# Subtracting the low part of every fourth weight chunk on GpSimd

## The chip, the cores and the metric

The kernel runs on one core of a Trainium2 chip. The time is device time in microseconds of one execution, compared by the median of several runs. Below, PE is TensorE (PEld its weight loads), DVE is VectorE, ACT is ScalarE, POOL is GpSimd and SP is SyncE, which issues the weight loads.

## What is computed

Two layers of an encoder over one sequence of 256 tokens of width 2048, in float32. Each layer has a mixer (an mLSTM group, a retention group and an attention group, side by side, from one projection of width 4432) and a feed-forward part of width 8192:

```
for l in range(DEPTH):
    h = _rms(x, g_mix[l])
    x = x + _mixer(h, cos, sin, w_in[l], ...)
    u = _rms(x, g_ffn[l])
    x = x + jnp.square(jax.nn.relu(u @ w_ff1[l])) @ w_ff2[l]
return _rms(x, g_final)
```

All weights together are some 390 MB, each read once. The matrix products dominate.

## The kernel before

**Split weights.** PE multiplies in a float32 form with fewer bits (`F32R`). To keep accuracy each operand is split in two: a high part, the value rounded to `F32R`, and a low part, the value minus the high part. Each product then has three matmuls: high by high, activation-high by weight-low, activation-low by weight-high. The activations are split once when they are made; the weights are split on the fly, and this is what the change is about.

**The weight stream.** `weight_plan` (line 47) lists all weights in the order in which PE wants them, and the host lays them out that way as 737 chunks, nearly all of 128 partitions by 1024 elements (512 KB). Class `Stream` (line 209) moves them. `load` (line 219) issues one DMA for a chunk on SP into one of `NRAW` = 4 raw buffers. `prep` (line 229) makes the two parts of chunk i: ACT copies the raw chunk to `whi` (line 237), DVE subtracts it from the raw chunk into `wlo` (line 238). There are `NHL` = 4 buffers of each, so chunk i has the buffers of chunk i - 4. After each `prep` the load of chunk i + 4 is issued, into the raw buffer that chunk i gives free; it waits for both the copy and the subtraction. `get(i)` (line 243), called when PE's code comes to chunk i, first calls `prep` up to chunk i + 2, so chunk i + 2's copy waits until PE has read the last of chunk i - 2 from the same buffer, and the two parts are made some two chunks ahead of their use.

**The order of the work.** Everything stands in the order in which the Python code emits it, engine by engine; no scheduler moves it. The main line of code runs the big products chunk by chunk: `nat` (line 411, weights as the moving operand), `stat` (line 416, weights as the stationary operand) and `ff_tile` (line 1066). All other work of the mixer (norms, gates, softmax, heads) is in generators that `pump` (line 379) advances by a step here and there between the matmuls. Each engine works off its queue in order, so a subtraction on DVE can stand behind an evacuation that waits for PE.

**The feed-forward part.** `ff1` (line 1082) takes four chunks for two tiles of 128 hidden units; each tile is evacuated by `ff_evac` (line 1052): ACT copies one half of the PSUM bank (line 1061), DVE adds the other (1062) and squares (1063), ACT and DVE split the result (325, 330). `ff2` (line 1099) takes four chunks for one block of 512 output columns, and `ev_x` (line 1034) adds the block to x on DVE. Per layer 32 ff1 groups and 32 ff2 blocks alternate, after four ff1 groups at the start and with four ff2 blocks at the end. A round is one ff1 group and one ff2 block, eight chunks. The feed-forward chunks begin at number 113 in layer 0 and 481 in layer 1, and every group of four begins at a number that leaves 1 when divided by 4.

**POOL.** It fills two buffers: `krl` at the start (line 291) and `rq` once in each layer (line 886). Nothing else stands in its queue besides a few constants.

Of the kernel before, what the change touches and what calls it, by code (L numbers as in the profile page):

```python
# [10 lines left out]
F32 = mybir.dt.float32  # L11
# [3 lines left out]
ALU = mybir.AluOpType  # L15
# [193 lines left out]
class Stream:  # L209
# [19 lines left out]
    def prep(self, upto):  # L229
        while self.nprep < min(upto, len(self.sizes)):  # L230
            i = self.nprep
            f = self.sizes[i]
            self.load(i + 1)
            raw = self.raw.pop(i)
            hi = self.pool.tile([P, CH], F32R, name=f"whi{i}", tag="whi", bufs=NHL)
            lo = self.pool.tile([P, CH], F32R, name=f"wlo{i}", tag="wlo", bufs=NHL)
            self.nc.scalar.activation(hi[:, :f], raw[:, :f], AF.Copy)  # L237
            self.nc.vector.tensor_tensor(lo[:, :f], raw[:, :f], hi[:, :f].bitcast(F32), op=ALU.subtract)  # L238
            self.parts[i] = (hi, lo)
            self.nprep += 1  # L240
            self.load(i + 1 + NRAW)
# [983 lines left out]
```

## Time and profile before

| | us |
|---|---|
| median of 3 runs | 2163.01 |
| lowest and highest | 2162.09 to 2163.02 |
| the profiled execution | 2164.72 |
| its span in the profile | 2162.9 |
| granted clock of PE, mean | 0.999 |

The profile lists busy time by engine, groups of equal instructions by source line ("L238 DVE ... wlo<-wraw,whi x737" is the subtraction), and for each group the idle time of its engine just before it and what ended that idle time. The timeline gives start and length of instructions, with equal neighbours merged ("x3"). Tile names are without buffer numbers; since chunks are copied, subtracted and used in order, the n-th instruction of line 237 or 238 belongs to chunk n, counted from 0.

### The profile page before, as it was taken

The numbers are of one execution on the slowest core, as the hardware profiler recorded it, in microseconds if no ns is written. First come the engines' busy times: TensorE is split into PE (matmuls) and PEld (weight loads), VectorE is DVE, ScalarE is ACT, GpSimd is POOL, SyncE is SP. The second block draws the span as 40 slices with busy tenths as digits, with TensorE's granted clock in tenths as the row PEclk, the third lists the DMA queues.
The fourth block names the chain that finished last, engine by engine and source line by source line (L and its number), as shares of the span: only waits on it lengthen the run. The fifth ranks groups of instructions, "written<-read, shape, count | busy, mean of one in ns | idle before, by whom it ended". The sixth has DMA issues, their size and how long they took to land.

```text
span 2162.9 us, 29276 instructions
## 1 busy us (share of the span) xinstructions
PE 2144.4 (99%) x11280; PEld 1837.5 (85%) x11280; DVE 1355.2 (63%) x2019; ACT 1047.5 (48%) x1534; POOL 4.1 (0%) x7
## 2 busy tenths in 40 slices
PE   8999999999999999999999999999999999999998
PEld 7898888888888888888888988888888888888887
DVE  5767565665656566565666676756565656656565
ACT  6645655544434444444556456555444444444444
POOL 0000000000000000000000000000000000000000
PEclk9999999999999999999999999999999999999999
DMA  7544455565565556565565444555555565555554
GB/s 212 186 144 159 153 175 185 175 199 190 189 200 179 202 185 196 187 202 179 188 185 171 131 166 137 186 183 193 187 191 199 179 203 183 197 187 201 177 204 164
DMA packets 111356, 395.20 MB, mean 183 GB/s; under 512 B 12904, under 2 KB 14056, under 8 KB 111088
## 3 DMA queue, kind: packets, MB, share of 16 engines
q1 hardware_dynamic: 109072, 389.90, 55.1%
q10 hardware_dynamic: 2144, 3.43, 0.4%
q8 instruction: 88, 1.44, 0.3%
q14 instruction: 52, 0.43, 0.1%
HBM read 391.17 MB, written 2.12 MB: 182 GB/s over the span
## 4 chain that ended last, share of the span: by engine, by line
PE 94%; DVE 2%; ACT 1%; DMA 1%; issue 1%; ACTq 0%; SPq 0%; DVEq 0%
PE pm L336 57%; PE f L336 33%; DMA wraw<-in_w_dram 1%; PE sc L336 1%; DVE wlo L238 1%; PE o L336 1%; ACT whi L237 1%; PE num L336 0%; PE xt L333 0%; PE ry L336 0%; PE pt L333 0%; PE st L336 0%; ACT junk L306 0%; DVE mqk L767 0%; DVE mqk L757 0%
## 5 line engine op out<-in xcount | busy, mean ns | idle before, releaser
L238 DVE TENSOR_TENSOR wlo<-wraw,whi 128x1024 fp32r<-128x1024 f32 (+2 forms) x737 | 875.0, 1217 | 269.8 <-ACT whi L237 268.2
L237 ACT ACTIVATE whi<-wraw 128x1024 fp32r<-128x1024 f32 (+2 forms) x737 | 750.5, 1048 | 332.8 <-PE pm L336 289.3
L336 PE MATMUL f<-xT,whi 128*128 128x512 f32 x2048 | 712.0, 392 | 0.0
L336 PE MATMUL f<-xT,wlo 128*128 128x256 f32 x2048 | 552.1, 280 | 0.0
L336 PEld LDWEIGHTS f<-xT,whi 128*128 128x128 f32 x2048 | 379.4, 188 | 77.0
L336 PE MATMUL pm<-wlo,hhi 128*128 128x512 f32 (+1 forms) x1040 | 401.6, 386 | 0.6 <-DVE wlo L238 0.6
L336 PE MATMUL pm<-whi,hhi 128*128 128x512 f32 (+1 forms) x1040 | 402.1, 387 | 0.0
L336 PE MATMUL pm<-whi,hlo 128*128 128x512 f32 (+1 forms) x1040 | 401.2, 386 | 0.0
L336 PEld LDWEIGHTS f<-xT,wlo 128*128 128x128 f32 x2048 | 385.0, 188 | 11.3 <-DVE wlo L238 0.8
L336 PE MATMUL pm<-whi,xT 128*128 128x512 f32 (+1 forms) x896 | 290.2, 393 | 2.3 <-ACT whi L237 1.8
L1061 ACT ACTIVATE fr<-f 128x256 f32<-128x256 f32 x128 | 49.2, 385 | 374.7 <-PE f L336 374.7
L336 PEld LDWEIGHTS pm<-wlo,hhi 128*128 128x128 f32 x1040 | 195.4, 188 | 40.3 <-DVE wlo L238 1.0
L336 PEld LDWEIGHTS pm<-whi,hlo 128*128 128x128 f32 x1040 | 195.4, 188 | 39.7
L336 PEld LDWEIGHTS pm<-whi,hhi 128*128 128x128 f32 x1040 | 195.4, 188 | 37.1
L336 PEld LDWEIGHTS pm<-whi,xT 128*128 128x128 f32 x896 | 166.7, 189 | 35.2 <-ACT whi L237 2.1
L1062 DVE TENSOR_TENSOR fr<-f,fr 128x256 f32<-128x256 f32 x128 | 54.3, 424 | 218.2 <-ACT fr L1061 218.2
L1034 DVE SCALAR_TENSOR_TENSOR xx<-pm,rs,xx 128x512 f32<-128x512 f32 x126 | 90.1, 750 | 143.1 <-PE pm L336 143.1
L336 PE MATMUL pm<-wlo,xT 128*128 128x512 f32 (+1 forms) x448 | 173.0, 386 | 3.5 <-DVE wlo L238 3.5
L325 ACT ACTIVATE hhi<-fq 128x256 fp32r<-128x256 f32 x128 | 53.5, 418 | 126.8 <-DVE fq L1063 126.8
L336 PEld LDWEIGHTS pm<-wlo,xT 128*128 128x128 f32 x448 | 84.6, 189 | 20.6 <-DVE wlo L238 5.8
L336 PE MATMUL pm<-whi,yhi 128*128 128x512 f32 x256 | 101.5, 397 | 0.0
L336 PE MATMUL pm<-whi,ylo 128*128 128x512 f32 x256 | 99.8, 390 | 0.0
(238 smaller groups left out, 1616.4 us busy)
## 6 DMA issues: line engine op xcount, KB each, us to landing
wraw<-in_w_dram SPq DMA_DIRECT2D x723, 512.0 KB, 4.2
wraw<-in_w_dram SPq DMA_DIRECT2D x10, 504.0 KB, 6.8
wt<-mx_rows ACTq DMA_DIRECT2D x8, 256.0 KB, 3.8
out_dram<-xx SPq DMA_DIRECT2D x8, 256.0 KB, 2.9
xx<-in_x_dram SPq DMA_DIRECT2D x3, 512.0 KB, 8.3
gf<-in_gfin_dram ACTq DMA_DIRECT2D x1, 1024.0 KB, 9.1
xx<-in_x_dram SPq DMA_DIRECT2D x2, 256.0 KB, 4.0
wraw<-in_w_dram SPq DMA_DIRECT2D x2, 256.0 KB, 5.3
```

Of the source, the lines that this page charges most:

```text
L237: self.nc.scalar.activation(hi[:, :f], raw[:, :f], AF.Copy)
L238: self.nc.vector.tensor_tensor(lo[:, :f], raw[:, :f], hi[:, :f].bitcast(F32), op=ALU.subtract)
L325: A.activation(hi, src, AF.Copy, **({"scale": g[0]} if g else {}))
L336: T.matmul(ps, lhsT=lhsT, rhs=rhs, start=start, stop=stop)
L1034: V.scalar_tensor_tensor(x[t][:, xs], ps[t], scale[:, t:t + 1], x[t][:, xs], op0=ALU.mult, op1=ALU.add)
L1061: A.activation(r, ps[:, S:], AF.Copy)
L1062: V.tensor_tensor(r, ps[:, :S], r, op=ALU.add)
```

## The change

Chunks whose number leaves 3 when divided by 4 have their low part subtracted on POOL; the instruction, its inputs and its output are the same. These are 184 of the 737 chunks.

```
             self.nc.scalar.activation(hi[:, :f], raw[:, :f], AF.Copy)
-            self.nc.vector.tensor_tensor(lo[:, :f], raw[:, :f], hi[:, :f].bitcast(F32), op=ALU.subtract)
+            eng = self.nc.gpsimd if i % 4 == 3 else self.nc.vector
+            eng.tensor_tensor(lo[:, :f], raw[:, :f], hi[:, :f].bitcast(F32), op=ALU.subtract)
             self.parts[i] = (hi, lo)
```

Later lines of the file move down by one. Since the buffers of a chunk are chosen by its number, one of the four `wlo` buffers is now written by POOL alone. PE's first matmul on such a low part, and the load into such a raw buffer, wait for POOL.

In the feed-forward part of layer 0, DVE's queue around the second block of ff2 in the third group stood as follows; chunks 205 to 208 are that block, 209 and 210 the first two of the next ff1 group, and `fr`, `fq`, `hlo` the evacuation of an ff1 tile.

```order
L238 TENSOR_TENSOR wlo205_5694<-wraw205_5606,whi205_5693 128x1024
L238 TENSOR_TENSOR wlo206_5716<-wraw206_5624,whi206_5715 128x1024
L1062 TENSOR_TENSOR fr_5737<-f_5692,fr_5737 128x256
L1063 SCALAR_TENSOR_TENSOR fq_5738<-fr_5737 128x256
L330 TENSOR_TENSOR hlo_5504<-fq_5738,hhi_5503 128x256
L238 TENSOR_TENSOR wlo207_5747<-wraw207_5645,whi207_5746 128x1024
L238 TENSOR_TENSOR wlo208_5765<-wraw208_5667,whi208_5764 128x1024
L238 TENSOR_TENSOR wlo209_5783<-wraw209_5697,whi209_5782 128x1024
```

In the changed kernel the same place on DVE, and then POOL's queue there:

```order
L239 TENSOR_TENSOR wlo205_5694<-wraw205_5606,whi205_5693 128x1024
L239 TENSOR_TENSOR wlo206_5716<-wraw206_5624,whi206_5715 128x1024
L1063 TENSOR_TENSOR fr_5737<-f_5692,fr_5737 128x256
L1064 SCALAR_TENSOR_TENSOR fq_5738<-fr_5737 128x256
L331 TENSOR_TENSOR hlo_5504<-fq_5738,hhi_5503 128x256
L239 TENSOR_TENSOR wlo208_5765<-wraw208_5667,whi208_5764 128x1024
L239 TENSOR_TENSOR wlo209_5783<-wraw209_5697,whi209_5782 128x1024
```

```order
L239 TENSOR_TENSOR wlo199_5567<-wraw199_5463,whi199_5566 128x1024
L239 TENSOR_TENSOR wlo203_5642<-wraw203_5570,whi203_5641 128x1024
L239 TENSOR_TENSOR wlo207_5747<-wraw207_5645,whi207_5746 128x1024
L239 TENSOR_TENSOR wlo211_5822<-wraw211_5750,whi211_5821 128x1024
L239 TENSOR_TENSOR wlo215_5927<-wraw215_5825,whi215_5926 128x1024
```

Chunk 207, the third of the ff2 block, has left DVE; on POOL it has nothing near it but the third chunks of the groups before and after.

At the end of the kernel, the last block of ff2 has chunks 733 to 736, and DVE's queue stood as follows; line 1034 is the evacuation of the block before, which waits for PE.

```order
L238 TENSOR_TENSOR wlo734_18498<-wraw734_18421,whi734_18497 128x1024
L1138 TENSOR_TENSOR xx_80<-xx_80,gf_18369 128x512 x2
L1034 SCALAR_TENSOR_TENSOR xx_80<-pm_18439,rs2_86,xx_80 128x512
L1034 SCALAR_TENSOR_TENSOR xx_80<-pm_18440,rs2_86,xx_80 128x512
L238 TENSOR_TENSOR wlo735_18518<-wraw735_18445,whi735_18517 128x1024
L238 TENSOR_TENSOR wlo736_18522<-wraw736_18463,whi736_18521 128x1024
```

In the changed kernel:

```order
L239 TENSOR_TENSOR wlo734_18498<-wraw734_18421,whi734_18497 128x1024
L1139 TENSOR_TENSOR xx_80<-xx_80,gf_18369 128x512 x2
L1035 SCALAR_TENSOR_TENSOR xx_80<-pm_18439,rs2_86,xx_80 128x512
L1035 SCALAR_TENSOR_TENSOR xx_80<-pm_18440,rs2_86,xx_80 128x512
L239 TENSOR_TENSOR wlo736_18522<-wraw736_18463,whi736_18521 128x1024
```

Chunk 735 no longer stands behind the evacuation; chunk 736 still does.

## The prediction

> **What bounds the kernel now.** I read the page's busy times first, then the waits of PE, then the timeline of one round of the feed-forward stage, and last the few places where PE stands still.
>
> ```profile
> PE 2144.4 (99%) x11280; PEld 1837.5 (85%) x11280; DVE 1355.2 (63%) x2019; ACT 1047.5 (48%) x1534; POOL 4.1 (0%) x7
> L238 DVE TENSOR_TENSOR wlo<-wraw,whi 128x1024 fp32r<-128x1024 f32 (+2 forms) x737 | 875.0, 1217 | 269.8 <-ACT whi L237 268.2
> L237 ACT ACTIVATE whi<-wraw 128x1024 fp32r<-128x1024 f32 (+2 forms) x737 | 750.5, 1048 | 332.8 <-PE pm L336 289.3
> 427.36:625.47 198.11, 198.11 (x1010) 169.11 (x1009) 119.98 (x144) 85.94 (x108) 0.00 (x0) 1.00 0.59 195
> 55.00:380.00 325.00, 324.57 (x1820) 281.57 (x1821) 216.54 (x402) 181.54 (x306) 1.81 (x1) 1.00 0.51 167
> 1140.00:1440.00 300.00, 297.31 (x1679) 257.95 (x1678) 198.46 (x367) 168.73 (x287) 1.81 (x1) 1.00 0.50 162
> 20.00:60.00 40.00, 35.49 (x182) 30.25 (x182) 24.84 (x68) 25.25 (x47) 0.00 (x0) 1.00 0.73 167
> ```
>
> ```profile
> PEld pm L336 <- DVE wlo L238: 9.2, 11, 1.3
> PE pm L336 <- DVE wlo L238: 5.5, 10, 1.0
> ```
>
> PE is busy for 2144.4 of 2162.9 us, at the full granted clock. In the stretch tables the columns after the length are PE, PEld, DVE, ACT and POOL. The first stretch is nine rounds of the feed-forward stage (22.01 us each: four chunks of ff1, four of ff2), and PE stands still for none of it. The next two are the mixers of the two layers: PE stands still for 0.43 and 2.69 us, while DVE is busy for 67 and 66%. The last is the start of layer 0, with 4.51 us. So DVE is no bound anywhere for long; taking 184 of its 737 subtractions (184 x 1.217 = 224 us) away shortens nothing by itself. The waits (second fence: us in total, times, longest) say the same: of 737 chunks, PE waited for the low part of some ten. The time can only change there, or where PE will wait for a low part that comes later.
>
> **The change: the price of one subtraction on POOL.** No row shows one. POOL has fills only:
>
> ```profile
> L886 POOL MEMSET rq<- 128x2048 f32 x2 | 3.6, 1812 | 1249.8 <-PE sc L336 1249.8
> L291 POOL MEMSET krl<- 128x256 f32 x1 | 0.3, 312 | 0.3 <-POOLq L1214 0.3
> ```
>
> From the two sizes, a stream costs (1812 - 312) / 1792 = 0.837 ns an element, with a start of 0.10 us. A subtraction over 1024 elements has two inputs and an output. One stream alone would be 0.96 us, two one after the other 1.81, all three 2.67; DVE takes 1.22. I take 2.24, the middle of two and three streams, as an estimate; 0.96 and 2.67 are the ends. The Trainium skill's GPSIMD Engine Reference, section "Performance versus the Vector engine", gives 4497 ns for a two-input fp32 operation of 2048 elements; half of that is an estimate of 2.25, by which the sum is the same, and it says that plain elementwise work belongs on VectorE.
>
> **The change: the 56 tight places.** In the feed-forward stage POOL gets the third chunk of each ff1 group and of each ff2 block. For ff1 there is time: chunk 211, copied at 640.09 in the round below, is read at 647.67. For ff2 there is less:
>
> ```profile
> 632.84 2.94 ACT L237 ACTIVATE whi<-wraw 128x1024 fp32r<-128x1024 f32 x3
> 632.97 0.43 DVE L330 TENSOR_TENSOR hlo<-fq,hhi 128x256 fp32r<-128x256 f32 x1 [0.48 <-ACT hhi L325]
> 633.92 3.50 DVE L238 TENSOR_TENSOR wlo<-wraw,whi 128x1024 fp32r<-128x1024 f32 x3 [0.53 <-ACT whi L237]
> 636.43 0.39 PE L336 MATMUL pm<-whi,hhi 128*128 128x512 f32 x1
> 636.66 0.39 PE L336 MATMUL pm<-wlo,hhi 128*128 128x512 f32 x1
> 631.14 10.89 PE pm L336 x48
> ...
> 647.67 0.28 PE L336 MATMUL f<-xT,wlo 128*128 128x256 f32 x1
> ```
>
> (The first rows are the timeline, with start and length in us; the row of 10.89 us is the ff2 block of four chunks in the chain of waits.) ACT is held back by the evacuation of an ff1 tile and copies three chunks in a row; the first of them, chunk 207 here, is ready at 633.9 and PE reads its low part at 636.66. The hand-over from the subtraction to PE is 0.05 us (at the end of the kernel, below: subtractions end at 2144.95, the matmul starts at 2145.00). That leaves 636.66 - 633.92 - 0.05 = 2.69 us, of which DVE uses 1.22 and POOL 2.24 by my price. The cover is the 0.45 us that remain; at 2.67 it is 0.02. Once it is gone every further tenth costs 28 interleaved ff2 blocks x 2 layers x 0.1 = 5.6 us, since PE has no idle time in a round to take it up. Here it costs nothing.
>
> What queues behind it: on SP the load into the raw buffer that the subtraction frees, and the later loads behind that one. It would be issued at about 636.2 in place of 635.2.
>
> ```profile
> wraw<-in_w_dram SPq DMA_DIRECT2D x723, 512.0 KB, 4.2
> 640.09 1.06 ACT L237 ACTIVATE whi<-wraw 128x1024 fp32r<-128x1024 f32 x1 [2.35 <-DMA wraw<-in_w_dram]
> 642.07 1.06 ACT L237 ACTIVATE whi<-wraw 128x1024 fp32r<-128x1024 f32 x1 [0.92 <-PE pm L336]
> ```
>
> That load ends the wait of the copy at 640.09 already; it moves to about 641.1 and ends at 642.2, so the next copy slips by 0.1 us. Both belong to ff1 chunks with over 5 us in hand: nothing. DVE, which no longer has chunk 207, can start chunk 208 when its high part is there, at 634.9.
>
> **The change: where PE waits directly behind a subtraction.**
>
> ```profile
> 392.87 2.36 DVE L238 TENSOR_TENSOR wlo<-wraw,whi 128x1024 fp32r<-128x1024 f32 x2 [0.53 <-ACT whi L237]
> 394.15 0.39 PE L336 MATMUL f<-xT,wlo 128*128 128x256 f32 x1
> 29.61 0.50 PE L336 MATMUL pm<-wlo,xT 128*128 128x512 f32 x1 [0.53 <-DVE wlo L238]
> 48.78 0.42 PE L336 MATMUL pm<-whi,xT 128*128 128x336 f32 x1 [1.78 <-ACT whi L237]
> 50.35 1.52 ACT L237 ACTIVATE whi<-wraw 128x336 fp32r<-128x336 f32 x2
> 53.80 2.35 DVE L238 TENSOR_TENSOR wlo<-wraw,whi 128x1024 fp32r<-128x1024 f32 x2
> 55.08 2.83 PE pm L336 x11
> 1147.35 1.22 DVE L238 TENSOR_TENSOR wlo<-wraw,whi 128x1024 fp32r<-128x1024 f32 x1 [0.27 <-ACT whi L237]
> 1159.39 0.50 PE L336 MATMUL pm<-wlo,chi 128*128 128x512 f32 x1 [0.60 <-DVE wlo L238]
> 2139.21 1.06 ACT L237 ACTIVATE whi<-wraw 128x1024 fp32r<-128x1024 f32 x1 [1.66 <-PE pm L336]
> 2141.93 1.06 ACT L237 ACTIVATE whi<-wraw 128x1024 fp32r<-128x1024 f32 x1 [1.66 <-PE pm L336]
> 2142.60 2.35 DVE L238 TENSOR_TENSOR wlo<-wraw,whi 128x1024 fp32r<-128x1024 f32 x2
> 2145.00 0.39 PE L336 MATMUL pm<-wlo,hhi 128*128 128x256 f32 x1 [0.15 <-DVE wlo L238]
> ```
>
> - Chunk 119, in the second ff1 group of layer 0, and its like in layer 1: DVE starts when the high part is there, and PE reads 0.06 us after it ends. 2.24 in place of 1.22 is paid in full: 2 x 1.02 = +2.0.
> - Chunk 7 (PE at 29.61) is as tight, +1.0; but at 48.78 PE waits 1.78 us for a copy whose load lands late, and that takes the delay up: 0, and +1.0 if that load moved as well.
> - Chunk 15: the high part is there at 51.87, DVE reaches the subtraction at 53.80, behind other work. POOL would end at 51.9 + 2.24 = 54.15 in place of 55.02: -0.9.
> - Chunk 391 (DVE at 1147.35) loses 1.0; chunks 392 to 394 follow it on a DVE queue that is short by 1.22, and PE waits for the last of them at 1159.39. Between -1.2 and +1.0; I take 0.
> - The last two chunks: chunk 735 is ready at 2140.27 and stood behind DVE's evacuation until 2142.60; on POOL it is done at 2142.5. Chunk 736 then starts when its high part ends, 2142.99, and is done at 2144.2 in place of 2144.95: -0.7.
> - The fill of line 886, at 181.6 now, comes to stand in POOL's queue behind chunk 67, whose high part is ready at 225.9: it would end at 225.91 + 2.24 + 1.81 = 230.0, its reader is at 236.7: 0.
>
> ```profile
> 225.91 1.23 DVE L238 TENSOR_TENSOR wlo<-wraw,whi 128x1024 fp32r<-128x1024 f32 x1 [5.40 <-ACT whi L237]
> L905 ACT ACTIVATE rq<-rt x8: 592/594/595, 236.7 to 1312.7; 64x512 f32<-64x512 f32 x8
> 181.56 1.81 POOL L886 MEMSET rq<- 128x2048 f32 x1 [180.52 <-PE sc L336]
> ```
>
> The sum is 2.0 + 0 - 0.9 + 0 - 0.7 = +0.4 us. For DVE work in the mixers that starts later because POOL reads beside it I add 1, so +1.4. The profiled execution took 2164.7 us (span 2162.9), 1.7 above the median of 2163.0; on the median it is 2164.4, and I say 2164.5.
>
> **A rule of the skill against it.** In the rows no subtraction runs beside POOL: its two fills of 1.81 us are all it did. The Trainium skill's page "SBUF — State Buffer", section "Who interferes with whom", says that a VectorE instruction with two SBUF inputs and a GpSimd instruction that reads SBUF exclude each other, and whichever starts first holds the other up until it ends. By that rule chunk 208 on DVE would wait from 634.9 to 636.2 and end at 637.4, wanted one chunk (10.89 / 4 = 2.72 us) after 636.66, at 639.4: nothing is lost in the feed-forward stage, and the sum stays. In the mixers it is a rival:
>
> **The rivals.**
> - *POOL is slowed by DVE at the tight places.* DVE's chunk 208 runs inside POOL's run there. If POOL loses the whole 1.22 us of it, it ends at 633.92 + 2.24 + 1.22 = 637.38, PE starts 0.77 late, 56 times: +43, with the two places like chunk 119 (again 1.22 each) +45.5: 2210. It decides once POOL needs over 2.69 us, so from 0.45 us of loss, or if my price is low by as much. For it: the margin is thin, and all 56 rounds look the same. Against it: POOL starts a microsecond earlier, and DVE is idle when it starts (its L330 row ended at 633.40). Chance 0.29.
> - *DVE is held up in the mixers.* 56 subtractions go to POOL there. Where DVE wants two inputs meanwhile it could stand still for up to 2.24 us while it saved 1.22, net 1.02 each. If a quarter of that reaches PE: 56 x 1.02 / 4 = +14: 2178. This is what the skill's rule of the shared interface would do. For it: DVE is busy two thirds of the time there. Against it: PE idles 0.43 us in 325, so the work of the side tasks comes in time, and DVE has 34 us less to do in each mixer. Chance 0.09.
> - *The relief reaches PE.* The idle time of PE in the mixers (0.43 + 2.69) and between 20 and 60 us (4.51, less 1.78 that a load causes) is 5.9 us at most. With most of it gone: 2158. Against it: at three of the places POOL itself is the later one. Chance 0.07.
>
> **How the numbers follow.** My forecast has 0.55. The three runs before lie within 1 us; I count a change over 0.2% (4.3 us) as one. Of the 0.55, 0.46 stays within that, 0.06 is above it by the unknown term of the mixers, 0.03 below by the ends of the terms (POOL at 0.96 us). Faster: 0.07 + 0.03 = 0.10. Same: 0.46. Slower: 0.29 + 0.09 + 0.06 = 0.44. The forecast's own range is 2159 to 2170; the range of 8 in 10 has to take in the first rival nearly whole, so 2159 to 2210.
>
> **What would show it.** In the changed profile: the POOL group of line 239, x184, mean near 2240 ns; PE as busy as before in a stretch of nine rounds, with rounds of 22.01 us; the matmul on chunk 119 about 1 us later behind its high part. I am wrong if the waits show PE held by POOL at an ff2 block's third chunk, if a round is longer than 22.1 us, or if PE's idle time in the mixers grows by more than 4 us.

## The result, and the profile after

The changed kernel takes 2177.61 us (median of 3 runs, 2177.18 to 2178.28) against 2163.01: 14.6 us slower, ratio 1.0069 (95% interval 1.0046 to 1.0092). The profiled execution took 2177.18 us with a span of 2175.4, so the two traces lie 12.5 us apart in their spans; the one of before was an execution 1.7 us above its median. The granted clock is 0.998 against 0.999. Two of the kernels measured later had one slow execution of eleven each (4354 and 6649 us), which their ratios leave out.

The page of the changed kernel: busy times, and the groups of the subtraction on both engines.

```profile
PE 2148.1 (99%) x11280; PEld 1839.1 (85%) x11280; DVE 1310.4 (60%) x1835; ACT 1046.6 (48%) x1534; POOL 450.6 (21%) x191
...
L239 DVE TENSOR_TENSOR wlo<-wraw,whi 128x1024 fp32r<-128x1024 f32 (+2 forms) x553 | 759.7, 1401 | 309.2 <-ACT whi L237 308.0
...
L239 POOL TENSOR_TENSOR wlo<-wraw,whi 128x1024 fp32r<-128x1024 f32 x184 | 446.6, 2427 | 1704.8 <-ACT whi L237 1640.9
```

DVE has 184 instructions of 1.217 us less, 224 us, but its busy time falls by only 44.8 (1355.2 to 1310.4). Its own remaining subtractions have grown from 1217 to 1401 ns in the mean. One on POOL takes 2427 ns in the mean. The same stretches of the changed kernel (length, then PE, PEld, DVE, ACT, POOL):

```profile
55.00:380.00 325.00, 320.96 (x1793) 277.19 (x1791) 215.39 (x374) 179.25 (x302) 62.73 (x26) 1.00 0.49 165
432.00:630.00 198.00, 198.00 (x1009) 169.13 (x1008) 113.64 (x127) 85.86 (x108) 43.32 (x18) 1.00 0.58 196
1150.00:1450.00 300.00, 293.57 (x1651) 254.19 (x1652) 194.33 (x331) 164.46 (x282) 58.84 (x24) 0.99 0.50 159
```

In nine feed-forward rounds PE still has no idle time, and a round still takes 22.01 us. In the mixers it now has 4.0 and 6.4 us, against 0.4 and 2.7. There DVE has lost 25 and 23 subtractions (30.4 and 28.0 us), but is busy only 1.2 and 4.1 us less: some 53 us have come back in the instructions that are left. Who PE waits for (us in total, times, longest):

```profile
PE pm L337 <- DVE wlo L239: 5.0, 4, 2.7
PE pm L337 <- POOL wlo L239: 3.0, 3, 1.6
PE pt L334 <- DVE pr L654: 2.7, 2, 1.4
PE krt L334 <- DVE kr L599: 2.4, 3, 1.6
PE f L337 <- POOL wlo L239: 2.3, 2, 1.1
```

Two of these are not about weights at all: `pt` transposes the attention probabilities, `krt` the rotated keys. PE did not wait for the first before, and for the second (L598 there) as below:

```profile
PE krt L333 <- DVE kr L598: 0.8, 2, 0.4
```

One place of each kind in the timeline of the changed kernel: POOL's chunk 23 and the DVE instruction beside it, chunk 55, and chunk 395 with the subtraction of chunk 394 that queues on DVE behind the held instruction.

```profile
74.22 2.36 POOL L239 TENSOR_TENSOR wlo<-wraw,whi 128x1024 fp32r<-128x1024 f32 x1 [10.18 <-ACT whi L237]
74.39 2.24 DVE L599 COPY kr<-kr 128x64 f32<-128x64 f32 x1
76.68 0.33 PE L334 MATMUL krt<-head,kr 128*128 128x128 f32 x1 [1.55 <-DVE kr L599]
...
187.68 2.37 POOL L239 TENSOR_TENSOR wlo<-wraw,whi 128x1024 fp32r<-128x1024 f32 x1 [12.80 <-ACT whi L237]
188.08 2.38 DVE L654 TENSOR_SCALAR pr<-pr,sm 128x256 f32<-128x256 f32 x2
190.25 0.81 PE L334 MATMUL pt<-head,pr 128*128 128x128 f32 x4 [1.37 <-DVE pr L654]
...
1162.33 2.76 POOL L239 TENSOR_TENSOR wlo<-wraw,whi 128x1024 fp32r<-128x1024 f32 x1 [7.88 <-ACT whi L237]
1162.88 2.49 DVE L728 TENSOR_SCALAR g_eu<-g_eu 4x512 f32<-4x512 f32 x1
1165.30 2.34 DVE L239 TENSOR_TENSOR wlo<-wraw,whi 128x1024 fp32r<-128x1024 f32 x2
1166.56 0.50 PE L337 MATMUL pm<-wlo,chi 128*128 128x512 f32 x1 [2.66 <-DVE wlo L239]
```

The timeline of the kernel before at the first and the last of these places:

```profile
76.26 0.20 DVE L598 COPY kr<-kr 128x64 f32<-128x64 f32 x1
...
1157.79 0.42 DVE L727 TENSOR_SCALAR g_eu<-g_eu 4x512 f32<-4x512 f32 x1
```

Each held instruction ends just after POOL's: 74.39 + 2.24 = 76.63 behind 74.22 + 2.36 = 76.58; 1162.88 + 2.49 = 1165.37 behind 1162.33 + 2.76 = 1165.09. A copy of 0.20 us took 2.24, and the next thing in line is PE.

At a tight place of the feed-forward stage the same happens, and costs nothing. POOL has the third chunk of an ff2 block and starts 0.90 us ahead of DVE's subtraction of the fourth; POOL keeps its 2.41 us, and the two subtractions of DVE take 3.72 in place of some 2.35:

```profile
638.34 2.41 POOL L239 TENSOR_TENSOR wlo<-wraw,whi 128x1024 fp32r<-128x1024 f32 x1 [12.63 <-ACT whi L237]
639.24 3.72 DVE L239 TENSOR_TENSOR wlo<-wraw,whi 128x1024 fp32r<-128x1024 f32 x2 [1.47 <-ACT whi L237]
```

Where the loss arises can be read from the start of PE's first matmul on each chunk, after minus before, and the steps of that difference along the stream:

| place (PE at chunk) | us | cause in the trace of after |
|---|---|---|
| 22 | +1.77 | DVE's L599 held by POOL's chunk 23 |
| 54 and 422 | +1.74, +1.74 | L654 held by chunks 55 and 423 |
| 60, 61 and 428, 429 | +0.94, +0.88 | DVE's queue behind L758, held by chunks 59 and 427 |
| 395 | +3.53 | L728 held by chunk 395, chunk 394's subtraction behind it (+2.06); half the granted clock (+1.47, below) |
| 392, 393 | +1.35, -0.77 | POOL's own subtraction of chunk 391, 2.53 us; part given back |
| 120 and 488 | +1.20, +1.21 | POOL's longer subtraction of chunks 119 and 487 |
| 8, 9 | +1.05, -0.66 | chunk 7, partly taken up |
| 13 | -1.67 | a load that landed earlier than in the trace of before |
| 16; the end | -0.77; -0.69 | chunk 15; the last two chunks |
| 47 and 415 | +0.46, +0.45 | L654 held by chunks 47 and 415 (156.46 to 158.52 at the first), PE just behind it |
| 84 | +0.16 | not explained |

The sum is +11.9 of 12.5. The step at chunk 13 does not belong to the change: it stands in about the same size in two kernels below in which no subtraction near it is on POOL (-1.58 and -1.59), and it is about what the profiled execution of before lay above its median.

The step at chunk 395 has two parts. PE waits 2.66 us there in place of 0.60, which is 2.06 of it. Then the granted clock is 0.50 for 3.41 us (the figure after the busy times in the stretch row below), and matmuls of 128x512 take 0.63 us in place of 0.39 and follow each other every 0.43 us in place of 0.23; the other 1.47 go there.

```profile
1167.44:1170.86 3.42, 3.42 (x10) 2.67 (x9) 0.20 (x1) 0.79 (x2) 0.00 (x0) 0.50 0.83 281
1168.13 0.63 PE L337 MATMUL pm<-whi,chi 128*128 128x512 f32 x1
```

The kernel below with only the mixer chunks on POOL has the same stretch (1167.37 to 1170.79). The one with nine chunks back on DVE, where PE waits 0.59 us there as before, has none between 11 and 2158 us. So the stretch goes with the long wait; that the wait brings it on is likely, not shown.

### The profile page after: what moved, and what is told of

Its sections match the earlier page's. It is cut to its first block, busy times and chain, and to the rows that moved or that the text cites. A ratio compares the mean times of both kernels' runs of the same rounds, so it can differ in the third digit from the quotient of the medians.

```text
span 2175.4 us, 29293 instructions
## 1 busy us (share of the span) xinstructions
PE 2148.1 (99%) x11280; PEld 1839.1 (85%) x11280; DVE 1310.4 (60%) x1835; ACT 1046.6 (48%) x1534; POOL 450.6 (21%) x191
## 4 chain that ended last, share of the span: by engine, by line
PE 92%; DVE 3%; ACT 2%; issue 1%; DMA 1%; POOL 0%; ACTq 0%; SPq 0%; DVEq 0%
PE pm L337 56%; PE f L337 31%; DVE wlo L239 1%; ACT whi L237 1%; PE sc L337 1%; DMA wraw<-in_w_dram 1%; PE xt L334 1%; PE num L337 0%; PE o L337 0%; PE pt L334 0%; DVE mqk L758 0%; DVE pr L654 0%; ACT junk L307 0%; POOL wlo L239 0%; PE ry L337 0%
## 5 line engine op out<-in xcount | busy, mean ns | idle before, releaser
L239 DVE TENSOR_TENSOR wlo<-wraw,whi 128x1024 fp32r<-128x1024 f32 (+2 forms) x553 | 759.7, 1401 | 309.2 <-ACT whi L237 308.0
L239 POOL TENSOR_TENSOR wlo<-wraw,whi 128x1024 fp32r<-128x1024 f32 x184 | 446.6, 2427 | 1704.8 <-ACT whi L237 1640.9
```

The costliest lines, as they stand in the source:

```text
L239: eng.tensor_tensor(lo[:, :f], raw[:, :f], hi[:, :f].bitcast(F32), op=ALU.subtract)
```

## The experiments

The theory was that POOL's subtraction and DVE's instructions on SBUF exclude each other, so that DVE's small instructions in the mixers end late, and that PE pays for some seven of them. The rival that the prediction had feared most was the feed-forward stage, where POOL's longer subtraction could be late at 56 places. For all experiments the kernel before was measured again on the same chip: 2163.44 us for the first four, 2163.40 for the last three. The edits shown leave out lines that only define names (`ff`, `cut`, the scratch tile `scr`) or choose the engine as the text says.

**Only the feed-forward chunks on POOL.**

```
+ ff = 113 <= i < 369 or i >= 481
- eng = self.nc.gpsimd if i % 4 == 3 else self.nc.vector
+ eng = self.nc.gpsimd if i % 4 == 3 and ff else self.nc.vector
```

> POOL takes every fourth chunk in the feed-forward stages only (128 of the 184). Theory (DVE is held up by POOL in the mixers): the 56 tight places cost nothing; two places like chunk 119 cost 1.2 us each, the last chunks gain 0.7: +1.7, 2164.7 us. Rival (each subtraction is late because it takes 2.41 us on POOL in place of 1.22, wherever it stands): 128/184 of the 14.6 us, 2173.

Measured: 2164.78 us, ratio 1.0006 (0.9997 to 1.0015). The steps of PE's starts are +1.19 at chunk 120, +1.19 at 488 and -0.70 at the last two chunks, and nothing else beyond the load at chunk 13. Chunks 119 and 487 are the whole price of 128 subtractions.

**Only the mixer chunks on POOL.**

```
+ eng = self.nc.gpsimd if i % 4 == 3 and not ff else self.nc.vector
```

> POOL takes every fourth chunk outside the feed-forward stages only (56 of the 184). Theory (DVE held up in the mixers): nearly the whole loss, +13, 2176 us, with DVE instructions of two SBUF inputs, or copies and tensor_scalars, stretched to over 2 us. Rival (late by POOL's own length): 56/184 of 14.6, 2167.5.

Measured: 2176.73 us, ratio 1.0063 (1.0049 to 1.0076). Its waits are those of the changed kernel:

```profile
PE pt L335 <- DVE pr L655: 2.7, 2, 1.4
PE krt L335 <- DVE kr L600: 2.4, 3, 1.6
```

56 subtractions make 13.3 of the 14.6 us. The loss is in the mixers.

**POOL busy beside DVE, but hardly reading.** All subtractions stay on DVE; for every fourth chunk POOL copies one column of the high part and then writes fills, whose results nobody uses.

```
+ if i % 4 == 3:
+     self.nc.gpsimd.tensor_copy(self.scr[:, :1], hi[:, :1].bitcast(F32))
+     for _ in range(15):
+         self.nc.gpsimd.memset(self.scr, 0.0)
```

> All subtractions stay on DVE. After the high part of every fourth chunk POOL reads one element a row of it and then does 15 fills of 128x64, about 2.4 us of POOL work that reads nothing and that nobody waits for. Theory (it is POOL's long read that holds DVE up): within 2 us of 2163. Rival (any POOL work beside DVE or ACT costs): over 2170.

Measured: 2163.77 us, ratio 1.0002 (0.9993 to 1.0011). Two groups of this kernel's page:

```profile
L240 DVE TENSOR_TENSOR wlo<-wraw,whi 128x1024 fp32r<-128x1024 f32 (+2 forms) x737 | 875.0, 1217 | 268.1 <-ACT whi L238 266.4
...
L244 POOL MEMSET dscr<- 128x64 f32 x2760 | 420.0, 152 | 158.5
```

POOL is busy as long as in the changed kernel (420 us of fills alone, against 447), and DVE's subtractions stay at 1217 ns to the digit: a POOL busy with short fills costs them nothing, so it matters what POOL does. These fills are of 0.15 us each, though, too short for a long hold to show. The profile of before has a fill of 1.81 us in each layer (line 886, 181.56 to 183.37 in the first), and beside it:

```profile
182.79 0.61 DVE L644 TENSOR_SCALAR mx<-mx 128x2 f32<-128x2 f32 x1
...
L644 DVE TENSOR_SCALAR mx<-mx x16: 168/170/626, 132.7 to 1253.9; 128x2 f32<-128x2 f32 x16
```

An instruction of 0.17 us took 0.61, until 183.40, where the fill ends, and 0.63 beside the second fill. In the changed kernel the fill lies elsewhere (231.32 to 233.13), and the subtraction that DVE starts beside it, at 232.06, takes its usual 1.22. So a long fill does hold this DVE instruction with one input, and not DVE's subtractions. This kernel therefore shows that the subtractions are free of fills; it does not show that a single long fill would leave the copies and TENSOR_SCALARs of the mixers alone. The other direction stands in the copies of one column (shortest, median and longest in ns):

```profile
L242 POOL COPY dscr<-whi x184: 183/1154/1273, 14.7 to 2138.8; 128x1 f32<-128x1 f32 x184
```

In 99 of the 184 cases a subtraction runs on DVE when the copy starts, or starts within 0.1 us; then the copy ends 0.04 to 0.05 us after that subtraction, and takes 1170 ns in the median. In the other 85 the median is 183, as is the mean in the kernel with late low parts below. Here it is POOL's read that waits for DVE's instruction.

**The same subtraction on POOL in eight pieces** (mixer chunks only).

```
+ n = 8 if cut else 1
+ for j in range(n):
+     s = slice(j * f // n, (j + 1) * f // n)
+     eng.tensor_tensor(lo[:, s], raw[:, s], hi[:, s].bitcast(F32), op=ALU.subtract)
```

> As the one with the mixers alone on POOL, but each subtraction on POOL is cut into 8 of 128 columns, with the same work and a total length on POOL of at least 2.4 us. Theory (DVE waits for the end of the POOL instruction that stands in its way): DVE is held for some 0.4 us at a time in place of 2.3, and most of the loss goes: 2167 (+4). Rival (the low part is late): no better than with whole subtractions, 2176 or more.

Measured: 2169.75 us, ratio 1.0031 (1.0020 to 1.0043), between the two: DVE's long holds go, as the theory has it, but POOL's low parts come late, as the rival has it. The timeline at the same place and before the v weights of layer 1, and the waits:

```profile
74.21 6.13 POOL L244 TENSOR_TENSOR wlo<-wraw,whi 128x128 fp32r<-128x128 f32 x8 [9.20 <-ACT whi L237]
74.38 0.34 DVE L604 COPY kr<-kr 128x64 f32<-128x64 f32 x1
...
1147.40 8.57 POOL L244 TENSOR_TENSOR wlo<-wraw,whi 128x128 fp32r<-128x128 f32 x8 [14.48 <-ACT whi L237]
...
1155.62 0.58 PE L342 MATMUL pm<-chi,wlo 128*128 128x256 f32 x1 [1.24 <-POOL wlo L244]
```

```profile
PE pm L342 <- POOL wlo L244: 6.6, 7, 1.7
...
PE krt L339 <- DVE kr L604: 0.8, 2, 0.4
```

The hold is as long as the piece: the copy takes 0.34 us, not 2.24, the wait of `krt` on DVE is down to 0.8 us and that of `pt` is gone. But now DVE gets in between the pieces and POOL pays: the subtraction of chunk 391 takes 8.57 us from first to last piece, and PE loses 5.26 us at chunk 392 alone: 3.20 are waits for the pieces, and the rest falls into a stretch of 6.83 us (from 1152.80) at a granted clock of 0.50. What DVE no longer loses, POOL does in part: 6.3 of the 13.3 us stay.

**The 56 tight places, with POOL started later.** As the first experiment, with a copy of one column and five fills ahead of each POOL subtraction.

```
+ if i % 4 == 3 and ff:
+     self.nc.gpsimd.tensor_copy(self.scr[:, :1], hi[:, :1].bitcast(F32))
+     for _ in range(5):
+         self.nc.gpsimd.memset(self.scr, 0.0)
```

> Only the feed-forward chunks (every fourth) have their low part on POOL, and each of these subtractions has a copy of one column and five fills of 128x64 ahead of it on POOL, whose results nobody reads. If the window of 2.69 us at the 56 tight places is as thin as worked out, 0.70 + 5 x 0.152 + 2.41 = 3.87 us put the low part 1.18 us late each time: +66 us, about 2230; up to 1.9 us late (+106, 2270) if VectorE's next subtraction, which now starts first, holds POOL up as well. At least +35 (2200) if the small operations overlap. Rival: the tight places are not thin, since PE or the other engines take the delay up within the block: about 2165, as with POOL's subtractions alone.

Measured: 2286.02 us, ratio 1.0565 (1.0550 to 1.0579), +122.6. The timeline at one tight place, and the waits:

```profile
658.61 0.18 POOL L242 COPY dscr<-whi 128x1 f32<-128x1 f32 x1 [10.56 <-ACT whi L238]
658.85 0.99 POOL L244 MEMSET dscr<- 128x64 f32 x5
659.52 5.67 DVE L245 TENSOR_TENSOR wlo<-wraw,whi 128x1024 fp32r<-128x1024 f32 x3 [1.47 <-ACT whi L238]
659.79 3.18 POOL L245 TENSOR_TENSOR wlo<-wraw,whi 128x1024 fp32r<-128x1024 f32 x1
663.03 0.50 PE L343 MATMUL pm<-wlo,hhi 128*128 128x512 f32 x1 [1.54 <-POOL wlo L245]
```

```profile
PE pm L343 <- POOL wlo L245: 87.0, 57, 1.6
PE f L343 <- POOL wlo L245: 14.8, 8, 3.1
```

A round grows from 22.01 to 23.85 us: 1.84 x 56 = 103, close to the upper of the two figures (106). The other 20 us arise at the first ff1 groups of the layers, four in each, where the low part is read as soon as it is there (second row of the waits, 14.8 us); some 3 us of it are matmuls at a granted clock of 0.50, for 3.41 us behind the first such wait in each layer. The expectation had left these groups out. POOL's subtraction begins 1.18 us after its high part instead of at once. A subtraction on DVE has started 0.27 us before it, and POOL takes 3.18 us, not 2.41. So the window is as thin as the prediction worked out, and the hold works here in POOL's disfavour; in the changed kernel POOL is the first to start, and DVE's subtraction, which has time, is the one that waits.

**Three places where DVE comes late.**

```
+ eng = self.nc.gpsimd if i in (15, 394, 735) else self.nc.vector
```

> Only chunks 15, 394 and 735 have their low part on POOL, three places where VectorE comes to the subtraction late behind other work. If each relief reaches PE: -0.8 (chunk 15), -0.6 to -1.2 (chunk 394) and -0.7 (the last two chunks), together about -2: 2161. Rival: VectorE is held up by POOL at these places as at the others, or the next wait takes the gain: 2163 to 2165.

Measured: 2164.38 us, ratio 1.0002 (0.9993 to 1.0011): the hoped 2 us are not there. The 0.70 at the last two chunks did come. At chunk 394 the timeline shows what was lost:

```profile
1152.29 2.41 POOL L239 TENSOR_TENSOR wlo<-wraw,whi 128x1024 fp32r<-128x1024 f32 x1 [969.82 <-ACT whi L237]
1152.35 3.57 DVE L712 TENSOR_TENSOR_SCAN g_eu<-g_ab 4x128 f32<-4x128 f32 x4
1155.85 1.19 DVE L239 TENSOR_TENSOR wlo<-wraw,whi 128x1024 fp32r<-128x1024 f32 x1
1157.09 0.50 PE L337 MATMUL pm<-wlo,chi 128*128 128x512 f32 x1 [2.19 <-DVE wlo L239]
```

DVE is rid of 1.22 us and held for 2.2: its four scans took 1.36 us before. PE waits for the subtraction of chunk 393 behind them, starts on chunk 394 2.23 us later against its neighbour, and gets 0.93 back at the next. What chunk 15 gives cannot be read from this profile: its wait is gone, but the granted clock is 0.50 from 49.72 to 53.13 us, just before PE comes to chunk 16, and PE loses 1.5 us there.

**Nine of the 184 back on DVE.**

```
+ eng = self.nc.gpsimd if i % 4 == 3 and i not in (23, 55, 59, 119, 391, 395, 423, 427, 487) else self.nc.vector
```

> As the changed kernel, but nine of its 184 chunks (23, 55, 59, 119, 391, 395, 423, 427, 487) keep their low part on VectorE. If the loss is made at these single places, where PE waits directly for the VectorE instruction that is held up or for POOL, 12 to 14 of the 14.6 us come back: 2163.5 to 2166. Rival: the loss is spread over all 184 (contention in general): 14.6 x 175/184 stays, 2177; if VectorE then is late at the neighbours in place of these, in between.

Measured: 2164.47 us, ratio 1.0002 (0.9993 to 1.0012). 175 subtractions stay on POOL, and the time is that of the kernel before. The subtraction's group on this kernel's page, and its waits:

```profile
L239 DVE TENSOR_TENSOR wlo<-wraw,whi 128x1024 fp32r<-128x1024 f32 (+2 forms) x562 | 771.3, 1400 | 307.0 <-ACT whi L237 305.7
```

```profile
PE pm L337 <- POOL wlo L239: 2.4, 3, 1.3
...
PE krt L334 <- DVE kr L599: 0.8, 2, 0.4
```

DVE is held elsewhere as in the changed kernel (1400 ns in the mean against 1401), and it costs little. The loss is made at these nine places; what the other 175 cost together is within the interval, 2.6 us at most.

## Why the prediction was right and wrong

The forecast was 2164.5 in a range of 2159 to 2210; 2177.6 lies in it by luck: the range was stretched for another case, the rival at the tight places. What happened is its second rival, at 2178 and a chance of 0.09, against 0.29 for the rival at the tight places and 0.55 for no change worth measuring.

- *The price on POOL*: 2.24 us was taken, with ends at 0.96 and 2.67; the median is 2.407. Counting streams by the fills gave the right size, 7% low, and the Trainium skill's estimate of 2.25 as well.
- *The tight places*: right, and by less than it looks. Of the 2.69 us the real price leaves 0.28. The kernel with the late start shows both that the window is real and that overrunning it costs 56 times. The rival failed at its condition that DVE slows POOL there: POOL starts 0.90 us earlier and keeps its 2.41.
- *Chunk 119 and its like*: +2.0 forecast, +2.41 measured, most of the difference being the 0.17 by which the price was low, twice. Chunk 15 -0.9 against -0.77, the last two chunks -0.7 against -0.69. Chunk 7 lost +1.05 as said and gave 0.66 back; the load at chunk 13 cannot be told apart from its own variation.
- *Chunk 391*: 0 was taken, within -1.2 and +1.0. It cost +0.58 (+1.35 and -0.77): inside the bounds.
- *The step that failed* is the sentence "For DVE work in the mixers that starts later because POOL reads beside it I add 1". By the table above this term is 1.77 + 3.48 + 1.82 + 3.53 = 10.6 us at six places (9.1 from DVE's late ends, 1.5 from the half clock behind the longest wait), and 0.9 more at chunks 47 and 415. The wording shows the slip: work that "starts later" was priced, and work that starts on time and ends late was not. The rival's condition was read off the wrong quantity, too. "PE idles 0.43 us in 325, so the work of the side tasks comes in time" says that the side tasks were never late by more than their margin; it does not say that the margin exceeds 2.2 us. At the L599 copy it is some 0.3: the copy took 2.04 us longer and PE came 1.77 late.
- *The rival's price* was near for a partly wrong reason. It let a quarter of the 1.02 us of every subtraction reach PE. Measured are some 53 us of holds in the mixers, of which some 10 reach PE, most of it at six places: nearly whole at four of them (1.7 to 2.1 us of 1.8 to 2.1), 0.9 of 2.0 at the two behind L758. Which subtractions these are is decided by what DVE has at hand when POOL starts.
- "DVE has 34 us less to do in each mixer" was no argument: its busy time there fell by 1.2 and 4.1 us.
- *The profile of before already had a hold.* The prediction says that in its rows no subtraction runs beside POOL, and names two fills of 1.81 us as all that POOL did. DVE's instructions beside them showed a hold of some 0.44 us each (0.61 and 0.63 for 0.17), on an instruction with one input.
- Of its own signs of being wrong the last one came: PE's idle time in the two mixers grew by 3.6 and 3.7 us, 7.3 together.

The rule that the prediction named, the Trainium skill's "SBUF — State Buffer", section "Who interferes with whom", describes what the rows show: held instructions end with POOL's subtraction, fills on POOL leave DVE's subtractions alone, and in the pieces and at the late start the order of starting decides who waits. The prediction weighed it only with a VectorE instruction of two inputs in mind; the same section also counts `copy` and `tensor_scalar` forms that use both of VectorE's ports, and the three held instructions shown above are of these two operations (L599, L654, L728).

Left open: whether a POOL instruction with a single input over 1024 elements, or one that only writes for 2.4 us, would hold the copies and TENSOR_SCALARs of the mixers as long was not tried; what makes the granted clock fall to 0.50 behind some of the waits is not shown; and the step at chunk 84 (0.16 us) stays unexplained.

## What to carry to other kernels

Work that goes from DVE to POOL can free far less of DVE than it takes over (here 44.8 of 224 us): count, for each moved instruction, the DVE instruction that will stand beside it and the margin of whoever waits for that one, down to copies of 0.2 us. Idle time of PE shows that nothing is late now, not by how much it could be; a hold of 2.4 us needs a margin of 2.4 us at every place. If such work has to move, choose the places one by one: here nine of 184 made nearly the whole loss.

## What the hardware showed beyond that

- Short instructions are held as long as long ones: 128x64 and 4x512 elements, 0.20 and 0.42 us alone, took 2.24 and 2.49.
- Cutting POOL's instruction into eight shortens the hold of DVE to 0.34 us, but lets DVE in between: 6.13 and 8.57 us for the eight pieces, against 2.41 in one.
- Fills on POOL of 0.15 us, 420 us of them, left DVE's 737 subtractions at 1217 ns. A fill of 1.81 us held a TENSOR_SCALAR of 128x2 elements to its own end, 0.61 us in place of 0.17.
- Behind PE's wait of 2.66 us the granted clock was 0.50 for 3.41 us, which cost 1.47 us on top of the wait.
